# Moving layer 2's modulation rows to other stages, the rotary multiplies to VectorE, and one weight split ahead of the block sums, in a two-layer backbone step

## The chip, the cores and the metric

The kernel runs on one core of a Trainium2 chip. Its engines work side by side, each through its own queue in order: TensorE (PE in the profile; PEld is its weight load), VectorE (DVE), ScalarE (ACT), GpSimd (POOL), and SyncE (SP), which here only issues transfers. The metric is the time of one execution on the device, in microseconds (us); lower is better. All data are float32.

## What is computed

One inference step of a backbone with two layers, width 1024, for 512 latent ("sample") and 128 context ("prompt") tokens. Layer 1 of the text (index 0) mixes with a gated DeltaNet and a long convolution, layer 2 (index 1) with two kinds of attention, one over all keys (mixer C, with normed q and k) and one over a window of 128 (mixer D). Each layer ends in a gated feed-forward net (ConvFFN) with 2816 inner channels. Every sub-layer takes a shift, a scale and a gate, the layer's six *modulations*, from the conditioning vector:

```python
def modulation(cvec, w_mod, b_mod):
    m = jax.nn.silu(cvec) @ w_mod + b_mod
    return jnp.split(m[:, None, :], 6, axis=-1)

def apply_rope_2d(x, cos, sin):
    ...
    out = jnp.stack([x1 * c - x2 * s, x2 * c + x1 * s], axis=-2).reshape(B, L, H, HD)

# each layer: x += gate * mixer(rmsnorm(x) * (1 + scale) + shift) @ w_out
#             x += gate * (silu(dwconv(h @ w_up_a)) * (h @ w_up_b)) @ w_dn
```

(The two comment lines sum up the trunk.) The six modulations of a layer are 6 x 1024 numbers for each of two conditioning vectors.

## The kernel before

The residual stream lies transposed in four tiles `x`, channels on partitions, 642 columns (both groups of tokens and two spare columns). Each float32 operand of a large product is split into a rounded high part and a rest (`split_w`: a copy on ScalarE gives `wwh`, a subtraction on VectorE `wwl`), and `mm3` (lines 307 to 311) sends three matmuls for every product: high by high (L309), high by rest (L310) and rest by high (L311). TensorE is thereby the engine with most work, and VectorE makes the rests it needs.

The stages come in this order: modulations of layer 1 and its mixers (to about 640 us of the span), layer 1's output projection, layer 1's feed-forward net in three groups (`FGROUPS`: 8, 7 and 7 tiles of inner channels), q/k/v projections of layer 2 by `od_unit`, attention, layer 2's output projection, layer 2's feed-forward net. A projection back to the residual is `project_out`: eight output tiles `d`, each in two column halves `out(d, w, hf)`, and behind each half `residual` (L445) on VectorE adds gate times result into `x`. Where a norm follows (`then`), the last four tiles' weights are split first and run half by half, with `sq` (ScalarE) and `acc` (L439, VectorE) adding up squares and `nr` (L394, GpSimd) taking the root.

**Modulation rows.** Layer 1's modulations are computed on TensorE at the start. Those of layer 2 are computed on VectorE by `mod_rows`, as multiply-and-accumulate instructions over 128x512 pieces (L256, `mjunk`) of the transposed weight (`mraw`, from `w_modT`), with the conditioning rows (`crow`) spread over partitions. Chunk `ch` of six is one of the modulations; a chunk is 32 such instructions. `mod_rows` is a generator: each `next` issues one piece of the load and its 4 (pieces of 1024) or 2 (pieces of 512) instructions. `LANES` says which chunks are made beside which stage. The pieces beside a `project_out` are drawn by its argument `between`, those beside the projections of layer 2 by the loop over `units(range(4))` (one piece in every third step), and those beside attention by `merge`, which interleaves generators by their costs; the last number of each of its pairs is the total cost a generator is taken for.

```python
LANES = (((0,), (1,), (2,)), (3, 4), (5,))     # groups of layer 1's FFN; layer 2's projections and attention; its output projection
```

**Rotation.** `od_post` is queued for each 128-token tile of q, k or v: a copy out of PSUM to `oy`, for mixer C a norm (ScalarE squares L1703, VectorE L1704, GpSimd root, VectorE L1709), and for q and k of latent tokens the rotary position: two multiplies of 128x128 elements into `ot` on GpSimd (L1718), one of 128x256 on VectorE (L1721), and the sum on VectorE (L1725). Then TensorE transposes the tile (L1734) and ScalarE copies it out. Each `yield` lets the steps of other tiles go first.

**Feed-forward start.** The net's input product is a block scheme on 2x2 blocks (seven products instead of eight) for all tiles but the first two, which run as `plain_unit`. Its operands are block sums made by `combine`; weights of a block tile are made by `block_weights` (loads, sums, and splits `cwh` on ScalarE, `cwl` on VectorE, L579/L580), one split for each `next`. The products of a block tile are named `bx`, `by`, `bv` after the PSUM bank they add into, those of a plain tile `pu`.

The program is written as one sequence; a scheduler then orders each engine's queue by readiness and priority, so what is written in another place may come out in another order on an engine. SP issues its loads strictly in its queue's order: a load whose buffer is still in use holds up the ones behind it.

## Time and profile before

| | us |
|---|---|
| median of three executions | 1896.49 |
| lowest, highest | 1892.93, 4376.39 |
| the profiled execution | 1896.52 |
| its span, first to last instruction | 1894.7 |

The span is what the profile shows; 1.8 us of that execution lie around it. The stages, by the times at which their lines run (us from the span's start):

| stage | from, to |
|---|---|
| layer 1's output projection | 640, 690 |
| layer 1's FFN: norm, two plain tiles, block tiles and three groups | 690, 1150 |
| layer 2's q/k/v projections of mixer C, with the norm and the rotation | 1150, 1222 |
| attention, with the projections of mixer D | 1222, 1380 |
| layer 2's output projection | 1380, 1424 |
| layer 2's FFN and final norm | 1424, 1895 |

In the profile a line such as "L1721 DVE ... x12 | 5.1, 425 | 8.7 <-POOL ot" is a group: 12 instructions of source line 1721 on VectorE, 5.1 us busy, 425 ns each on average, and 8.7 us in which the engine sat idle just before them, waiting for GpSimd's `ot`. Rows of waits say which instruction of which engine was waited for, the total, the number of times and the longest. Rows of the timeline give start, duration, engine, line, and in brackets the idle time before and who ended it. PEclk is the clock that TensorE was granted, as a share of full speed. Buffer numbers are left out of names.

### The profile page before, as it was taken

The numbers are of one execution on the slowest core, as the hardware profiler recorded it, in microseconds if no ns is written. First come the engines' busy times: TensorE is split into PE (matmuls) and PEld (weight loads), VectorE is DVE, ScalarE is ACT, GpSimd is POOL, SyncE is SP. The second block draws the span as 40 slices with busy tenths as digits, with TensorE's granted clock in tenths as the row PEclk, the third lists the DMA queues.
The fourth block names the chain that finished last, engine by engine and source line by source line (L and its number), as shares of the span: only waits on it lengthen the run. The fifth ranks groups of instructions, "written<-read, shape, count | busy, mean of one in ns | idle before, by whom it ended". The sixth has DMA issues, their size and how long they took to land. (4 is left out here: it accounts for less than half of the span.)

```text
span 1894.7 us, 31530 instructions
## 1 busy us (share of the span) xinstructions
PE 1790.8 (95%) x12052; PEld 1666.0 (88%) x12052; DVE 1366.1 (72%) x2848; ACT 846.6 (45%) x1676; POOL 338.5 (18%) x397
## 2 busy tenths in 40 slices
PE   5899999999889999999999998899999999999998
PEld 1578899998667899999989998877899999999997
DVE  4755666667887759777777888796777873774774
ACT  3555443433232346624624635444536651552653
POOL 2313432324554100000000004310001000000001
PEclk9899999999989999999999999999999999999999
DMA  8322112224544613564564554431242461552631
GB/s 283 124 98 91 34 58 73 66 69 140 173 167 148 200 51 81 156 191 123 143 190 130 161 174 154 145 116 35 96 167 73 129 156 57 142 144 76 158 93 56
DMA packets 86929, 233.15 MB, mean 123 GB/s; under 512 B 9176, under 2 KB 20824, under 8 KB 86650
## 3 DMA queue, kind: packets, MB, share of 16 engines
q1 hardware_dynamic: 66976, 191.40, 30.8%
q0 software_dynamic: 5760, 20.97, 6.7%
q10 hardware_dynamic: 14042, 18.76, 2.8%
q8 instruction: 95, 1.56, 0.3%
q14 instruction: 56, 0.46, 0.1%
HBM read 214.56 MB, written 16.54 MB: 122 GB/s over the span
## 5 line engine op out<-in xcount | busy, mean ns | idle before, releaser
L579 ACT CAST cwh<-wr 128x512 fp32r<-128x512 f32 x200 | 119.6, 620 | 152.4 <-PE bx L310 43.6
L303 ACT CAST wwh<-wr 128x1024 fp32r<-128x1024 f32 (+1 forms) x100 | 101.3, 1013 | 182.7 <-PE mm L310 116.0
L580 DVE TENSOR_TENSOR cwl<-wr,cwh 128x512 fp32r<-128x512 f32 x200 | 133.4, 686 | 39.1 <-ACT cwh L579 38.8
L445 DVE SCALAR_TENSOR_TENSOR x<-mm,mod,x 128x128 f32<-128x128 f32 (+3 forms) x192 | 77.4, 435 | 107.8 <-PE mm L311 107.7
L304 DVE TENSOR_TENSOR wwl<-wr,wwh 128x1024 fp32r<-128x1024 f32 (+1 forms) x100 | 122.1, 1223 | 44.1 <-ACT wwh L303 43.4
L309 PE MATMUL mm<-h0h,wwh 128*128 128x384 f32 (+2 forms) x448 | 148.8, 332 | 0.5 <-DVE d L845 0.2
L591 POOL DMA_DIRECT2D t<-in_w_up x40 | 35.0, 874 | 604.9 <-DMA t<-in_w_up 248.5
L310 PE MATMUL mm<-h0l,wwh 128*128 128x384 f32 (+2 forms) x448 | 140.3, 313 | 0.0
L311 PE MATMUL mm<-h0h,wwl 128*128 128x384 f32 (+2 forms) x448 | 139.4, 311 | 0.0
L256 DVE SCALAR_TENSOR_TENSOR mjunk<-mraw,crow 128x512 f32<-128x512 f32 x192 | 126.7, 691 | 6.0 <-DMA mraw<-in_w_modT 5.7
L309 PE MATMUL od<-owh,h2h 128*128 128x256 f32 x320 | 97.3, 307 | 0.6 <-ACT h2h L428 0.6
L679 DVE SCALAR_TENSOR_TENSOR cv<-ab,par,cv 128x641 f32<-128x641 f32 x88 | 77.7, 883 | 26.3 <-ACT cv L677 25.5
L311 PE MATMUL od<-owh,h2l 128*128 128x256 f32 x320 | 91.3, 289 | 2.2 <-DVE h2l L429 1.3
L310 PE MATMUL od<-owl,h2h 128*128 128x256 f32 x320 | 91.8, 288 | 0.4 <-DVE owl L1613 0.4
L1134 POOL TENSOR_TENSOR am<-a,msk 128x512 fp32r<-128x512 f32 x60 | 72.8, 1221 | 92.4 <-PE Q L1163 81.2
L309 PEld LDWEIGHTS mm<-h0h,wwh 128*128 128x128 f32 x448 | 85.4, 191 | 3.1 <-issue 1.8
L310 PEld LDWEIGHTS mm<-h0l,wwh 128*128 128x128 f32 x448 | 84.9, 190 | 0.6 <-issue 0.2
L311 PEld LDWEIGHTS mm<-h0h,wwl 128*128 128x128 f32 x448 | 84.6, 189 | 0.1
L721 DVE SCALAR_TENSOR_TENSOR cv<-mm,par,cv 128x382 f32<-128x382 f32 (+2 forms) x96 | 52.1, 544 | 32.8 <-ACT cv L715 32.0
L436 ACT ACTIVATE sq<-x 128x320 f32<-128x320 f32 (+4 forms) x63 | 31.5, 501 | 83.8 <-DVE x L445 75.8
L579 ACT CAST cwh<-t 128x512 fp32r<-128x512 f32 x80 | 48.1, 623 | 41.7 <-PE bx L310 17.4
L310 PEld LDWEIGHTS od<-owl,h2h 128*128 128x128 f32 x320 | 61.4, 192 | 4.3 <-issue 3.6
(556 smaller groups left out, 6184.1 us busy)
## 6 DMA issues: line engine op xcount, KB each, us to landing
wr<-in_w_mod SPq DMA_DIRECT2D x48, 512.0 KB, 4.6
wr<-in_w_up SPq DMA_DIRECT2D x48, 512.0 KB, 4.1
t<-in_w_up SPq DMA_DIRECT2D x80, 256.0 KB, 3.2
t<-in_w_up POOLq DMA_DIRECT2D x40, 512.0 KB, 6.4
mraw<-in_w_modT SPq DMA_DIRECT2D x32, 512.0 KB, 5.1
wr<-in_w_in SPq DMA_DIRECT2D x28, 512.0 KB, 3.3
wr<-in_w_dn SPq DMA_DIRECT2D x32, 448.0 KB, 3.4
wr<-in_w_up SPq DMA_DIRECT2D x40, 256.0 KB, 3.5
```

Of the source, the lines that this page charges most:

```text
L256: nc.vector.scalar_tensor_tensor(out=junk, in0=w[:, c : c + 512], scalar=1.0, in1=rows[m][:, c0 + c : c0 + c + 512], op0=ALU.mult, op1=ALU ...
L303: nc.scalar.copy(hi[:, :K], src)
L304: nc.vector.tensor_tensor(out=lo[:, :K], in0=src, in1=hi[:, :K].bitcast(F32), op=ALU.subtract)
L309: nc.tensor.matmul(ps, l[0](k), r[0](k), start=start, stop=False, skip_group_check=more)
L310: nc.tensor.matmul(ps, l[0](k), r[1](k), start=False, stop=False, skip_group_check=more)
L311: nc.tensor.matmul(ps, l[1](k), r[0](k), start=False, stop=stop, skip_group_check=more)
L445: nc.vector.scalar_tensor_tensor(out=xt[:, a:b], in0=ps[:, a - c0 : b - c0], scalar=mcol(layer, ch, d, m), in1=xt[:, a:b], op0=ALU.mult, o ...
L579: nc.scalar.copy(hi, src)
L580: nc.vector.tensor_tensor(out=lo, in0=src, in1=hi.bitcast(F32), op=ALU.subtract)
L679: nc.vector.scalar_tensor_tensor(out=t[:, c0:c1], in0=ar[:, c0 + s_ : c1 + s_], scalar=w[i], in1=t[:, c0:c1], op0=ALU.mult, op1=ALU.add)
L721: nc.vector.scalar_tensor_tensor(out=t[:, c0:c1], in0=p[:, c0 + s_ - a : c1 + s_ - a], scalar=w[i], in1=t[:, c0:c1], op0=ALU.mult, op1=ALU ...
L1134: eng.tensor_tensor(out=v(out), in0=v(a32), in1=msk[:, lv, :, None, :].broadcast_to([P, 2, 2, P]), op=ALU.mult)
```

## The change

Five edits that the diff shows, of which the first two decide where a row of modulations is made:

- `LANES` becomes one list for all stages. Layer 1's output projection, which had no such work, makes chunk 0; the three groups of layer 1's FFN make chunks 1, 2 and 3; attention makes chunk 4 only; layer 2's output projection makes chunk 5, as before. The loop that drew pieces during `units(range(4))` is gone.
- `project_out` draws a piece after a tile's two halves and no longer ahead of its weights (where there is no norm behind, it drew two pieces ahead of each of the first two tiles); in the last four tiles it draws one after the first half's product.
- The two rotary multiplies run on VectorE; `oy` has six buffers, `ot` one.
- Every tile waits one step more ahead of its transposes (only q of mixer C did).
- In the feed-forward start, the third tile's `block_weights` and its first two splits stand between the two `combine` calls' parts, and that tile's `up_unit` is called inside the branch.

```diff
@@ -1,5 +1,6 @@
 import math
 from contextlib import ExitStack
+from itertools import chain
 
 import numpy as np
 
@@ -61,7 +62,7 @@
 RATE = 1.0
 
 
-LANES = (((0,), (1,), (2,)), (3, 4), (5,))
+LANES = ((0,), ((1,), (2,), (3,)), (4,), (5,))
 
 
 PCOL = {}
@@ -476,18 +477,17 @@
 
         first = KD - 4 if then else KD
         for d in range(first):
-            for _ in range(2 if d < 2 and not then else 1):
-                next(between, None)
             w = ws[d] if d < len(ws) else split_w(load_raw(wsrc(d), K), K)
             for hf in range(2):
                 out(d, w, hf)
+            next(between, None)
 
         ws = [split_w(load_raw(wsrc(d), K), K) for d in range(first, KD)]
         for hf in range(2):
             for d, w in zip(range(first, KD), ws):
+                q = out(d, w, hf)
                 if hf == 0:
                     next(between, None)
-                q = out(d, w, hf)
                 if hf == 1 and d == first:
                     norm_stats(acc, rb, 0, cut=cut)
                 if hf == 1 and d == first + soon:
@@ -622,7 +622,7 @@
                 yield
         give(f, ar, br, 1.0)
 
-    def up_unit(layer, f, B, pool, outs, give):
+    def up_unit(layer, f, B, pool, outs, give, ws=None):
 
 
         def product(ps, n, st):
@@ -635,7 +635,7 @@
             nc.scalar.copy(q, ps[:, :ST])
             return q
 
-        ws = block_weights(layer, f, pool)
+        ws = ws or block_weights(layer, f, pool)
         ar, br = (outs[f % 2][:, i, :] for i in range(2))
         X, Y = bank("d", "bx"), bank("mm", "by")
         product(X, "a11", True)
@@ -693,10 +693,15 @@
                 us = [plain_unit(*pre[2 * f : 2 * f + 2], f, B, outs, give) for f in range(2)]
                 for u in us:
                     next(u)
-                for k, u in zip((0, 2), us):
-                    combine(B, k)
-                    next(u, None)
-                f1 = 2
+                combine(B, 0)
+                next(us[0], None)
+
+                ws = block_weights(layer, 2, pool)
+                early = [next(ws) for _ in range(2)]
+                combine(B, 2)
+                next(us[1], None)
+                up_unit(layer, 2, B, pool, outs, give, chain(early, ws))
+                f1 = 3
             for f in range(f1, f0 + n):
                 up_unit(layer, f, B, pool, outs, give)
             project_out(
@@ -1597,7 +1602,7 @@
         B = Blocks(gstack.enter_context(tc.tile_pool(name=f"g{layer}", bufs=8)))
         pool = gstack.enter_context(tc.tile_pool(name=f"b{layer}", bufs=2))
         take, pre = to_blocks(x, layer, B)
-        between = rows_beside(LANES[2], pool) if layer else iter(())
+        between = rows_beside(LANES[3 * layer], pool)
         project_out(x, mix, layer, 2, wout(layer), KD, take, between=between, ws=ws, cut=SCUT, soon=3)
         return B, pool, gstack, pre
 
@@ -1632,7 +1637,7 @@
             for i in range(4):
                 nc.scalar.dma_start(xs[:, 2 * i : 2 * i + 2, :], x[i])
 
-    ffn_blocks(x, B, bpool, 0, to_attention, None, gstack, pre, LANES[0])
+    ffn_blocks(x, B, bpool, 0, to_attention, None, gstack, pre, LANES[1])
     h = h2
 
 
@@ -1694,7 +1699,7 @@
             if t == 4:
                 nc.sync.dma_start(O["new_v"][mixer], dst)
             return
-        y = od.tile([P, 256], F32, tag="oy", name=nm("oy"), bufs=5)
+        y = od.tile([P, 256], F32, tag="oy", name=nm("oy"), bufs=6)
         nc.scalar.copy(y, ps)
         if mixer == 0:
             sq = tmp.tile([P, NT], F32, tag="fs", name=nm("osq"))
@@ -1711,11 +1716,11 @@
                     in1=gains[:, 0 if part < 2 else 1, :], op0=ALU.mult, op1=ALU.mult,
                 )
         if t < 4:
-            t2 = od.tile([P, 256], F32, tag="ot2", name=nm("ot2"))
+            t2 = od.tile([P, 256], F32, tag="ot2", name=nm("ot2"), bufs=1)
             q4 = lambda ap: ap.rearrange("p (h g x c) -> p h g x c", h=2, g=2, x=2)
             r4 = lambda ap: ap.rearrange("p (g x c) -> p g x c", g=2, x=2)[:, None].broadcast_to([P, 2, 2, 2, 32])
             for i in range(2):
-                nc.gpsimd.tensor_tensor(
+                nc.vector.tensor_tensor(
                     out=q4(t2)[:, :, :, i, :], in0=q4(y)[:, :, :, 1 - i, :], in1=r4(rope[:, 1, t, :])[:, :, :, i, :], op=ALU.mult
                 )
             nc.vector.tensor_tensor(
@@ -1727,8 +1732,7 @@
             nc.sync.dma_start(O["new_k"][mixer], y)
         yield
         yield
-        if u < 2:
-            yield
+        yield
         pt = s_ps("ot")
         for i in range(2):
             nc.tensor.transpose(pt[:, BLK[i]], y[:, BLK[i]], ident)
@@ -1970,12 +1974,10 @@
                     yield c
 
     lanes = mod_rows(
-        LANES[1], lambda: od.tile([P, 1024], F32, tag="crow", name=nm("crow")),
+        LANES[2], lambda: od.tile([P, 1024], F32, tag="crow", name=nm("crow")),
         lambda: od.tile([P, 512], F32, tag="mraw", name=nm("mraw"), bufs=3), 512,
     )
-    for n, _ in enumerate(units(range(4))):
-        if n % 3 == 2:
-            next(lanes)
+    run(units(range(4)))
     lend["by"] = None
     att["pool"] = odv.enter_context(tc.tile_pool(name="att", bufs=2))
     identb = att["pool"].tile([P, P], BF16, tag="identb", name="identb", bufs=1)
@@ -1989,7 +1991,7 @@
             pattern=[[s_, P]], channel_multiplier=-s_,
         )
     att_all = all_heads()
-    merge((units((4, 6, 7, 5)), 54.0), (until_none(att_all), AW), (lanes, 29.5))
+    merge((units((4, 6, 7, 5)), 54.0), (until_none(att_all), AW), (lanes, 24.8))
     lend["by"] = "attention"
     for _ in att_all:
         step()

```

What the scheduler makes of it is seen in each engine's order. On SP, in the second group of layer 1's FFN: `mraw` are the modulation pieces, `wr<-in_w_dn` the output projection's weights. Before:

```order
L298 DMA wr_9863<-in_w_dn 128x896
L298 DMA wr_9926<-in_w_dn 128x896
L251 DMA mraw_9603<-in_w_modT 128x1024
L251 DMA mraw_9664<-in_w_modT 128x1024
L251 DMA mraw_9672<-in_w_modT 128x1024
L251 DMA mraw_9733<-in_w_modT 128x1024
L251 DMA mraw_9794<-in_w_modT 128x1024
L251 DMA mraw_9855<-in_w_modT 128x1024
L251 DMA mraw_9916<-in_w_modT 128x1024
L298 DMA wr_9979<-in_w_dn 128x896
L298 DMA wr_10032<-in_w_dn 128x896
```

and now (line numbers are one higher):

```order
L299 DMA wr_9911<-in_w_dn 128x896
L299 DMA wr_9972<-in_w_dn 128x896
L252 DMA mraw_9781<-in_w_modT 128x1024
L252 DMA mraw_9842<-in_w_modT 128x1024
L252 DMA mraw_9903<-in_w_modT 128x1024
L299 DMA wr_10033<-in_w_dn 128x896
L252 DMA mraw_9964<-in_w_modT 128x1024
L252 DMA mraw_10025<-in_w_modT 128x1024
L299 DMA wr_10094<-in_w_dn 128x896
L252 DMA mraw_10086<-in_w_modT 128x1024
```

Before, seven modulation loads in a row stood ahead of the last two weight loads; now no more than three stand ahead of the next weight.

On VectorE, in layer 1's output projection, around the weight of its fourth tile: `x<-mm` is the residual (`mm_6288` and `mm_6315` are the halves of the first tile before), `acc` the sum of squares, `wwl` the rest of a weight (`wwl_6470` is the fourth tile's before). Before:

```order
L304 TENSOR_TENSOR wwl_6405<-wr_6402,wwh_6404 128x1024
L445 SCALAR_TENSOR_TENSOR x_6272<-mm_6288,mod,x_6272 128x320
L445 SCALAR_TENSOR_TENSOR x_6272<-mm_6315,mod,x_6272 128x192
L445 SCALAR_TENSOR_TENSOR x_6272<-mm_6315,mod,x_6272 128x128
L304 TENSOR_TENSOR wwl_6470<-wr_6467,wwh_6469 128x1024
L304 TENSOR_TENSOR wwl_6535<-wr_6532,wwh_6534 128x1024
L445 SCALAR_TENSOR_TENSOR x_6272<-mm_6343,mod,x_6272 128x320
L439 TENSOR_TENSOR acc_6286<-acc_6286,sq_6369 128x320
L445 SCALAR_TENSOR_TENSOR x_6272<-mm_6372,mod,x_6272 128x192
L445 SCALAR_TENSOR_TENSOR x_6272<-mm_6372,mod,x_6272 128x128
L304 TENSOR_TENSOR wwl_6541<-wr_6538,wwh_6540 128x1024
```

and now, where `mm_6430` and `mm_6459` are the halves of the third tile and `wwl_6500` is the fourth tile's rest:

```order
L446 SCALAR_TENSOR_TENSOR x_6273<-mm_6430,mod,x_6273 128x320
L257 SCALAR_TENSOR_TENSOR mjunk_6421,mpart<-mraw_6416,crow_6344 128x512
L440 TENSOR_TENSOR acc_6286<-acc_6286,sq_6456 128x320
L257 SCALAR_TENSOR_TENSOR mjunk_6491,mpart<-mraw_6489,crow_6343 128x512
L257 SCALAR_TENSOR_TENSOR mjunk_6494,mpart<-mraw_6489,crow_6343 128x512
L257 SCALAR_TENSOR_TENSOR mjunk_6491,mpart<-mraw_6489,crow_6344 128x512
L446 SCALAR_TENSOR_TENSOR x_6273<-mm_6459,mod,x_6273 128x192
L446 SCALAR_TENSOR_TENSOR x_6273<-mm_6459,mod,x_6273 128x128
L257 SCALAR_TENSOR_TENSOR mjunk_6494,mpart<-mraw_6489,crow_6344 128x512
L440 TENSOR_TENSOR acc_6286<-acc_6286,sq_6486 128x322
L305 TENSOR_TENSOR wwl_6500<-wr_6497,wwh_6499 128x1024
```

The fourth tile's rest stood behind the first tile's residuals; now it stands behind the third tile's second residual, a modulation instruction and a sum, that is, behind work that the third tile's last matmuls set free.

On VectorE, in layer 2's projections, one tile's norm and rotation. Before:

```order
L256 SCALAR_TENSOR_TENSOR mjunk_12052,mpart<-mraw_12050,crow_11827 128x512
L1721 TENSOR_TENSOR oy_11990<-oy_11990,rope 128x256
L256 SCALAR_TENSOR_TENSOR mjunk_12052,mpart<-mraw_12050,crow_11828 128x512
L1725 TENSOR_TENSOR oy_11990<-oy_11990,ot_2086_12037 128x256
L1709 SCALAR_TENSOR_TENSOR oy_12041<-oy_12041,ors_12048,gains 128x128 x2
L1704 TENSOR_SCALAR oss_12094<-oss_12094 128x2
L256 SCALAR_TENSOR_TENSOR mjunk_12115,mpart<-mraw_12113,crow_11827 128x512
L1721 TENSOR_TENSOR oy_12041<-oy_12041,rope 128x256
L256 SCALAR_TENSOR_TENSOR mjunk_12115,mpart<-mraw_12113,crow_11828 128x512
L1725 TENSOR_TENSOR oy_12041<-oy_12041,ot_2095_12087 128x256
```

and now:

```order
L1723 TENSOR_TENSOR ot_2094_12037<-oy_12000,rope 128x4x32 x2
L1714 SCALAR_TENSOR_TENSOR oy_12041<-oy_12041,ors_12048,gains 128x128
L1726 TENSOR_TENSOR oy_12000<-oy_12000,rope 128x256
L1709 TENSOR_SCALAR oss_12095<-oss_12095 128x2
L1709 TENSOR_SCALAR oss_12140<-oss_12140 128x2
L1730 TENSOR_TENSOR oy_12000<-oy_12000,ot_2094_12037 128x256
L1714 SCALAR_TENSOR_TENSOR oy_12092<-oy_12092,ors_12099,gains 128x128
L1723 TENSOR_TENSOR ot_2104_12088<-oy_12041,rope 128x4x32 x2
L1714 SCALAR_TENSOR_TENSOR oy_12092<-oy_12092,ors_12099,gains 128x128
L1726 TENSOR_TENSOR oy_12041<-oy_12041,rope 128x256
```

The modulation pieces between the steps are gone, and the pair of multiplies that GpSimd made stands on VectorE (L1723). Chunk 4's 32 instructions stand further on: one ahead of the first tile and three among the rotated tiles, then 18 almost without a break in the rows where unit 3 runs (the v tiles, which have neither norm nor rotation), with the splits of unit 4's weights (`owl`) at the end of that stretch, and 10 among the attention's.

## The prediction

> **What bounds the kernel now.** I read the page first (busy times), then the windows by stage, then the waits of TensorE in each window, and the timelines around the longest of them.
>
> ```profile
> PE 1790.8 (95%) x12052; PEld 1666.0 (88%) x12052; DVE 1366.1 (72%) x2848; ACT 846.6 (45%) x1676; POOL 338.5 (18%) x397
> ```
> TensorE is busy 95% of the span, and the change takes no matmul away. It can only move the remaining 5%, some 104 us, together with matmuls that run at a lower clock. So I look where the edits touch, for TensorE's waits and its granted clock.
>
> ```profile
> core 0: us, PE busy (x) PEld busy (x) DVE busy (x) ACT busy (x) POOL busy (x), PEclk, DMA share, GB/s
> 640.00:705.00 65.00, 62.37 (x408) 60.88 (x408) 36.93 (x72) 25.02 (x44) 3.36 (x7) 0.97 0.35 119
> 973.00:979.00 6.00, 2.58 (x8) 2.58 (x9) 6.00 (x18) 0.00 (x0) 0.00 (x0) 0.76 0.61 206
> 1170.00:1222.00 52.00, 42.33 (x320) 39.34 (x321) 41.77 (x126) 23.94 (x87) 28.11 (x44) 0.97 0.33 107
> 1222.00:1340.00 118.00, 113.02 (x729) 90.73 (x728) 90.29 (x278) 53.39 (x145) 12.13 (x22) 0.99 0.27 86
> 1472.00:1482.00 10.00, 6.63 (x29) 6.37 (x28) 9.24 (x17) 4.37 (x8) 0.00 (x0) 0.66 0.06 23
> ```
> Four places leave TensorE idle: one stall in the feed-forward net's second group (973), layer 2's projections (9.67 us idle of 52), attention (4.98 of 118) and one stall at layer 2's feed-forward start (1472). Layer 1's output projection has VectorE at 37 of 65 us: there is the room that the change fills.
>
> **The second group's stall (973).**
>
> ```profile
> 971.46 0.28 PE L310 MATMUL mm<-g01l,wwh 128*128 128x258 f32 x1
> 976.42 0.69 PE L311 MATMUL mm<-g01h,wwl 128*128 128x384 f32 x1 [4.67 <-DVE wwl L304]
> ...
> 979.46 0.37 PE L311 MATMUL mm<-g01h,wwl 128*128 128x384 f32 x1
> 979.67 0.34 PE L309 MATMUL mm<-g01h,wwh 128*128 128x384 f32 x1
> 979.85 0.34 PE L310 MATMUL mm<-g01l,wwh 128*128 128x384 f32 x1
> ```
> ```profile
> 956.33 19.39 SPq L251 DMA_DIRECT2D mraw<-in_w_modT  x7
> 976.39 3.78 SPq L298 DMA_DIRECT2D wr<-in_w_dn  x2
> ```
> TensorE waits for a weight's rest, which stands on VectorE behind modulation instructions; seven modulation loads hold SP from 956 to 976 with two weight loads behind them. From start to start the gap is 976.42 - 971.46 = 4.96, where 0.12 is usual: 4.8 lost. After it ten matmuls start in 979.67 - 976.42 = 3.25 us, where ten steps of 0.18 (979.67 to 979.85) make 1.8: 1.45 more at the lower clock. In the new order no weight stands behind more than three modulation loads, and each weight's split stands on VectorE at least one tile ahead of its use. The cover is that one tile of matmuls; without it the next weight would stall likewise. I take -6.0 of the 6.25 (bounds: 0, if another weight is late instead, and -6.25).
>
> At this place the Trainium skill (TensorE: Matmul & The Clock Gate, "HAM oscillation") says that an idle gap of more than about 3.4 us halves TensorE's clock, for about 3.4 us of work. This agrees with the rows here on when it happens, a wait of 2.47 us without and of 3.37 and 4.67 us with slow matmuls behind it (rows below and above). It would price each at 1.7 us, an estimate from that page, where the rows give 1.45 here and 2.4 below; by the page the sum would come out 0.45 us higher.
>
> **Layer 2's projections (1170 to 1222).**
>
> ```profile
> PE ot L1734 <- DVE oy L1725: 5.0, 6, 1.4
> PE ot L1734 <- ACT osq L1703: 2.0, 2, 1.1
> L256 DVE SCALAR_TENSOR_TENSOR mjunk<-mraw,crow 128x512 f32<-128x512 f32 x25 | 17.2, 694 | 0.0
> L1709 DVE SCALAR_TENSOR_TENSOR oy<-oy,ors,gains 128x128 f32<-128x128 f32 x30 | 9.6, 346 | 1.5 <-POOL ors L193 1.5
> L1721 DVE TENSOR_TENSOR oy<-oy,rope 128x256 f32<-128x256 f32 x12 | 5.1, 425 | 8.7 <-POOL ot L1718 8.7
> L1704 DVE TENSOR_SCALAR oss<-oss 128x2 f32<-128x2 f32 x14 | 2.5, 191 | 0.0
> L1718 POOL TENSOR_TENSOR ot<-oy,rope 128x128 f32<-128x128 f32 x24 | 16.5, 709 | 14.9 <-DVE oss L1704 14.5 <-DVE oy L1709 0.4
> 1198.03 0.28 PE L309 MATMUL od<-owh,h2h 128*128 128x256 f32 x1
> 1198.14 0.28 PE L310 MATMUL od<-owl,h2h 128*128 128x256 f32 x1
> ```
> Transposes wait for a chain: VectorE's norm, GpSimd's pair of multiplies (2 x 0.71 us), VectorE again, with modulation instructions between. VectorE itself idles 8.7 us for GpSimd. Undisturbed, a matmul starts about every 0.118 us, so the window's 320 need 37.8 us and 14.2 of its 52 are lost. Other waits of that list, for splits and copies out, make 3.0 and stay; 11.2 hang on the chain.
>
> Of the edits, the loop's removal takes up to 25 modulation instructions off (17.2 us of VectorE); the pair costs VectorE 24 multiplies of 128x128, which the trace does not show on it. The nearest row is L1709 of that size, 0.346 with a scalar operand: 0.35 each, 8.4 us (bounds: 0.2, the L1704 row of two columns, and 0.43, L1721 of twice the size). A rotated tile then costs VectorE 0.19 + 2 x 0.35 + 2 x 0.35 + 0.43 + 0.43 (L1725, as L1721) = 2.45 us against 24 x 0.118 = 2.83 us of matmuls: VectorE keeps up. One step more before the transposes costs TensorE nothing, since matmuls of the next tile stand there; it needs the sixth `oy`. The wait for GpSimd's root stays. I take -11 (bounds: 0, if the modulation burst behind the rotated tiles makes up new waits, to -14.2).
>
> **Attention (1222 to 1340).**
>
> ```profile
> PE tr L1004 <- ACT oy L1698: 2.4, 1, 2.4
> L256 DVE SCALAR_TENSOR_TENSOR mjunk<-mraw,crow 128x512 f32<-128x512 f32 x40 | 27.8, 708 | 4.0 <-DMA mraw<-in_w_modT 3.8
> L1721 DVE TENSOR_TENSOR oy<-oy,rope 128x256 f32<-128x256 f32 x11 | 4.6, 418 | 6.1 <-POOL ot L1718 4.5 <-ACT mxh L1763 1.6
> 1252.66 0.62 DVE mjunk L256 x2
> 1253.30 3.08 DMA mraw<-in_w_modT
> ```
> The last two rows are of the chain that ended last, which at this place runs through modulation instructions on VectorE and the load of one. Of 40, ten remain: 30 x 0.71 = 21 us less; 22 multiplies of 0.35 = 7.7 us more; the waits for GpSimd (4.5) go. But most of this is beside other work: TensorE idles 4.98 us, and 1% of clock is 1.2. I take -4 of these 6.2 (bounds -6.2 and +3: the ten instructions and eleven pairs stand ahead of softmax steps on VectorE that TensorE's transposes wait for, 10 x 0.71 + 7.7 = 15 us, of which a fifth may show).
>
> **The feed-forward starts.**
>
> ```profile
> 734.54 0.41 PE L311 MATMUL by<-a12h,cwl 128*128 128x320 f32 x1 [2.47 <-DVE cwl L580]
> 714.00:741.00 27.00, 24.53 (x168) 24.24 (x167) 26.77 (x43) 18.63 (x34) 0.00 (x0) 1.00 0.04 13
> 1475.73 0.63 PE L311 MATMUL bx<-a11h,cwl 128*128 128x320 f32 x1 [3.37 <-DVE cwl L580]
> ...
> 1481.23 0.33 PE L309 MATMUL bx<-s2h,cwh 128*128 128x320 f32 x1
> 1481.84 0.31 PE L310 MATMUL bx<-s2l,cwh 128*128 128x320 f32 x1
> 1481.99 0.31 PE L311 MATMUL bx<-s2h,cwl 128*128 128x320 f32 x1
> ```
> In layer 1 VectorE is busy 26.77 of the 27 us: it does combinations and splits without a pause. Taking two splits forward moves the combinations back by as much, so the 2.47 wait stands at another product of the same tile: 0 (bounds -2.5, +1). In layer 2 the wait is the tile's very first split: 3.37, after which 21 matmuls take 1481.23 - 1475.73 = 5.5 us, where 21 x 0.147 = 3.1. The first two splits now lie ahead; the later wait should be that of layer 1, 2.5, short of what brought the low clock: -(3.4 - 2.5) - 2.4 = -3.3 (bounds 0 and -5.8).
>
> **Layer 1's output projection: what is added.**
>
> ```profile
> L304 DVE TENSOR_TENSOR wwl<-wr,wwh 128x1024 fp32r<-128x1024 f32 x9 | 11.0, 1220 | 5.7 <-ACT wwh L303 5.6
> L445 DVE SCALAR_TENSOR_TENSOR x<-mm,mod,x 128x320 f32<-128x320 f32 (+2 forms) x20 | 8.4, 447 | 12.1 <-PE mm L311 12.0
> L439 DVE TENSOR_TENSOR acc<-acc,sq 128x320 f32<-128x320 f32 (+1 forms) x11 | 5.4, 491 | 4.4 <-ACT sq L436 4.4
> L256 DVE SCALAR_TENSOR_TENSOR mjunk<-mraw,crow 128x512 f32<-128x512 f32 x32 | 20.7, 686 | 1.9 <-DMA mraw<-in_w_modT 1.9
> PE rb L402 <- POOL nr L394: 0.3, 1, 0.3
> PE rb L402 <- POOL nr L394: 0.9, 1, 0.9
> ```
> (The first three rows are of 640 to 690, the fourth of layer 2's output projection, where the same 32 instructions already run without holding TensorE; the last two are the norm behind each projection, layer 1's first.) VectorE has 65 - 37 = 28 us for 20.7. But the fourth tile's rest now stands behind the third tile's second residual: two pieces of residual (0.9), one modulation instruction (0.7), a sum (0.5) and the rest itself (1.2) pass after that tile's last matmul, 3.3 us, while eight matmuls that need only high parts go ahead (1.2): +2.1. The transfers `t` of the block tiles move behind the modulations on SP and POOL, as in layer 2 already; there the root `nr` on GpSimd stands behind an accumulating transfer, and its wait is 0.9 instead of 0.3: +0.6. Eight modulation loads and two of `crow` go past four `x` and four weight loads on SP; they are hidden, since the fourth weight is needed six half tiles (6 x 24 x 0.147 = 21 us) after the first. Together +2.7 (bounds 0 and +9: if a modulation load lands late on VectorE's queue, each weight behind it waits as at 973, 6.25). Groups one and three and layer 2's output projection, with as much work as before in nearly the same order: 0.
>
> **Sum.** -6.0 - 11 - 4 - 3.3 + 0 + 2.7 = -21.6; against the profiled execution's 1896.5 that is 1874.9. Its span is 1894.7 with 1.8 around it, and it lies within 0.1 of the median of 1896.49, so I take the sum for the median too. About 2% (38 us) is what a measurement of this kernel can tell from no change; the forecast lies inside.
>
> **Rivals.**
> - *Waits only move.* The 18 modulation instructions in a row (14 us with their reads) run as fast as their loads land through three buffers; a load of this kind cost VectorE 3.08 in one place. Behind them stand the splits of the next unit's weights, so TensorE waits there, and the projections gain 3, attention 0: -6 - 3 - 3.3 + 2.7 = -9.6, 1886.9. For it: VectorE's queue is in order; against it: v tiles leave VectorE nothing else to do.
> - *All goes.* Projections -14.2, attention -6.2, both starts -2.5 and -5.8, the added work hidden: -6.25 - 14.2 - 6.2 - 8.3 = -35, 1861.5. Against it: VectorE's own instructions in the third window (41.8 - 17.2 + 8.4 = 33 of 52 us) must then hide wholly. The Trainium skill (SBUF — State Buffer, "Who interferes with whom") has GpSimd and VectorE lock each other out at a shared port, so that VectorE would get time back for each multiply taken off GpSimd. The rows agree little: `mjunk` takes 694 ns beside the multiplies and 686 in layer 2's output projection without them.
> - *Layer 1's output projection becomes the stall.* Its weights come through the same SP queue as eight new loads. If the five weights four to eight each wait as the one at 973 (6.25), that is +31 in place of +2.7, and the whole is +7: 1903.5. It decides from four late weights on (25 against the 24.3 gained). Against it: the new order lets no more than four modulation loads stand ahead of a weight.
> - *Rotation makes VectorE the bound* (0.43 for each multiply and 25 modulation instructions still in that window): the window stays at 52 us, attention +3, total -6 + 3 - 3.3 + 2.7 = -3.6, 1892.9.
>
> **Chances.** Forecast 0.52 (its own range 1867 to 1883), waits only move 0.20, all goes 0.12, rotation the bound 0.06, output projection the stall 0.10. The range 1860 to 1893 holds all but the last and tails, 8 in 10 and a little more. Faster by over 2% (below 1858.6) needs more than all the bounds: 0.04. Slower by over 2% (above 1934.4) needs more than five such weights: 0.02. Within 2%: 0.94.
>
> **What would show it.** No `wwl` wait near the second group's fifth tile, and PEclk 1.00 there; no `ot` waits for `oy` in the projections and no GpSimd rows of the rotation; TensorE's wait at layer 2's feed-forward start below 3 us at full clock, and layer 1's still near 2.5; a new wait of about 2 us for `wwl` in layer 1's output projection. I am wrong if VectorE's 18 instructions in a row are followed by a wait of TensorE for `owl`, if a multiply on VectorE takes over 0.45 us, or if layer 1's output projection shows several waits for weights.

## The result, and the profile after

| | before | with the change |
|---|---|---|
| median, us | 1896.08 (4 executions) | 1879.21 (4, from 1878.37 to 1880.43) |
| span of the profiled execution, us | 1894.7 | 1878.7 |

The ratio is 0.9908, 95% interval 0.9889 to 0.9926: about 17 us (14 to 21) less, inside the 2%, with an interval that is clear of no change. Of the four executions before, one took 4376.39 us, and the ratio is taken without it. The forecast was 1874.9, in a range of 1860 to 1893. A second measurement of the same kernel gave 0.9922 (0.9898 to 0.9946).

The same views as before, of the changed kernel: the page's busy times, windows at the places that correspond, and TensorE's waits there. Line numbers are one to five higher.

```profile
PE 1788.3 (95%) x12052; PEld 1665.0 (89%) x12052; DVE 1374.1 (73%) x2896; ACT 848.1 (45%) x1678; POOL 311.4 (17%) x349
```
```profile
core 0: us, PE busy (x) PEld busy (x) DVE busy (x) ACT busy (x) POOL busy (x), PEclk, DMA share, GB/s
967.00:973.00 6.00, 6.00 (x43) 6.00 (x42) 5.86 (x17) 0.87 (x1) 0.00 (x0) 1.00 0.57 183
1165.60:1209.00 43.40, 40.29 (x325) 38.33 (x324) 37.55 (x124) 23.15 (x89) 16.00 (x21) 1.00 0.31 100
1209.00:1327.00 118.00, 113.99 (x731) 91.72 (x730) 83.21 (x262) 53.67 (x147) 0.40 (x1) 0.97 0.19 61
1459.00:1467.00 8.00, 5.93 (x29) 5.40 (x28) 8.00 (x15) 3.68 (x7) 0.00 (x0) 0.79 0.04 13
```
```profile
PE tr L1009 <- ACT oy L1703: 3.7, 1, 3.7
...
PE bv L312 <- DVE cwl L580: 3.6, 2, 1.8
...
PE mm L312 <- DVE wwl L305: 2.0, 1, 2.0
...
PE ot L1738 <- DVE oy L1730: 1.5, 3, 0.6
...
PE ot L1738 <- ACT osq L1708: 0.6, 1, 0.6
```
The reader is to see three things. The second group's stall is gone: TensorE is busy 6.00 of 6.00 us at full clock. Layer 2's projections take 43.4 us for what took 52, with 2.1 us of waits for `oy` and `osq` in place of 7.0. And at attention's start the wait for `oy`, 2.4 us before, is now 3.7, at a granted clock of 0.97 (0.99 before), although VectorE has 7 us less to do there than before (83.21 against 90.29).

To see where the time went I use that TensorE runs the same 12,052 matmuls in every trace. A stage is the time from the start of one numbered matmul to that of another, read from TensorE's timeline, so that a stage can be compared wherever it lies in the span. Some matmuls stand in another order after an edit, so a stage's bounds can lie a few matmuls off.

| stage, by its time in the span before | before | change | change, second profile |
|---|---|---|---|
| start, 4 to 133 | 129.4 | 125.2 | 129.9 |
| layer 1's mixers, 133 to 531 | 397.7 | 397.6 | 397.8 |
| their last part, 531 to 600 | 68.6 | 70.3 | 65.1 |
| up to layer 1's output projection and through it, 600 to 681 | 81.6 | 84.5 | 82.2 |
| norm and plain tiles, 681 to 722 | 40.8 | 40.4 | 40.8 |
| layer 1's feed-forward start, 722 to 762 | 40.0 | 42.3 | 41.2 |
| groups one and two, 762 to 955 | 193.5 | 193.7 | 192.3 |
| second group's output, 955 to 988 | 32.8 | 26.4 | 26.4 |
| third group, norm, 988 to 1161 | 173.1 | 173.2 | 174.0 |
| layer 2's projections, 1161 to 1229 | 67.9 | 58.5 | 58.5 |
| attention, 1229 to 1380 | 150.8 | 150.2 | 148.9 |
| layer 2's output projection and norm, 1380 to 1450 | 70.6 | 69.8 | 70.6 |
| layer 2's feed-forward start, 1450 to 1496 | 45.7 | 43.9 | 42.4 |
| the rest, 1496 to 1884 | 387.3 | 386.8 | 387.7 |

Two profiles of one program differ by 4.7 us at the start and by 5.2 us in the last mixer part, which the edits do not touch; what the table shows there is no effect of the change. The rest is: 6.3 less at the second group, 9.4 less in the projections, 2 to 3 less at layer 2's feed-forward start, 1 to 2 more at layer 1's, 1 to 3 more around layer 1's output projection, and 1 to 2 less at attention.

### The profile page after: what moved, and what is told of

Read it like the earlier page. It is cut to its first block, busy times and chain, and to the rows that moved or that the text cites. A ratio compares the mean times of both kernels' runs of the same rounds, so it can differ in the third digit from the quotient of the medians.

```text
span 1878.7 us, 31471 instructions
## 1 busy us (share of the span) xinstructions
PE 1788.3 (95%) x12052; PEld 1665.0 (89%) x12052; DVE 1374.1 (73%) x2896; ACT 848.1 (45%) x1678; POOL 311.4 (17%) x349
## 4 chain that ended last, share of the span: by engine, by line
PE 72%; DVE 13%; ACT 3%; POOL 3%; issue 2%; DMA 2%; POOLq 0%; DVEq 0%; ACTq 0%
PE mm L310 10%; PE mm L312 10%; PE mm L311 10%; PE bx L310 4%; PE bx L311 4%; PE bx L312 4%; PE bv L312 2%; PE bv L310 2%; PE bv L311 2%; PE tr L1009 2%; PE fx L1395 1%; PE YT L1176 1%; PE Y L1174 1%; PE Q L1168 1%; PE o L1872 1%
## 5 line engine op out<-in xcount | busy, mean ns | idle before, releaser
L305 DVE TENSOR_TENSOR wwl<-wr,wwh 128x1024 fp32r<-128x1024 f32 (+1 forms) x100 | 122.2, 1223 | 39.4 <-ACT wwh L304 38.6
L1139 POOL TENSOR_TENSOR am<-a,msk 128x512 fp32r<-128x512 f32 x60 | 73.0, 1225 | 92.4 <-PE Q L1168 81.2
L312 PEld LDWEIGHTS mm<-h0h,wwl 128*128 128x128 f32 x448 | 84.5, 189 | 0.1
L310 PEld LDWEIGHTS od<-owh,h2h 128*128 128x128 f32 x320 | 60.4, 189 | 4.5 <-issue 4.2
```

Source lines behind the costliest of these rows:

```text
L305: nc.vector.tensor_tensor(out=lo[:, :K], in0=src, in1=hi[:, :K].bitcast(F32), op=ALU.subtract)
L310: nc.tensor.matmul(ps, l[0](k), r[0](k), start=start, stop=False, skip_group_check=more)
L312: nc.tensor.matmul(ps, l[1](k), r[0](k), start=False, stop=stop, skip_group_check=more)
L1139: eng.tensor_tensor(out=v(out), in0=v(a32), in1=msk[:, lv, :, None, :].broadcast_to([P, 2, 2, P]), op=ALU.mult)
```

## The experiments

Stage lengths in us, as in the table above; each run is one profile. "Draw order" is `project_out`'s edit, "placement" the edits of `LANES` and of the draws beside the projections and attention. The experiments come from three chips, on which the kernel before took 1892.35, 1896.67 and 1898.33 us, so total times are compared as ratios to it, and a difference between stages counts for little where two profiles of the change differ by as much (2.3 us at the output projection, 1.5 at layer 2's start, 1.3 at attention).

| run | output projection (600 to 681) | layer 1's start | second group | projections | attention | layer 2's start |
|---|---|---|---|---|---|---|
| before | 81.6 | 40.0 | 32.8 | 67.9 | 150.8 | 45.7 |
| the change | 84.5 | 42.3 | 26.4 | 58.5 | 150.2 | 43.9 |
| rotation back on GpSimd | 84.4 | 41.1 | 26.4 | 60.9 | 158.1 | 43.9 |
| third tile undone | 82.1 | 43.0 | 26.4 | 58.5 | 150.1 | 44.9 |
| draw order alone | 81.6 | 40.2 | 26.4 | 66.4 | 152.7 | 44.9 |
| rotation and third tile alone | 82.3 | 40.6 | 32.9 | 60.1 | 147.0 | 43.9 |
| draw order and rotation | 81.8 | 39.4 | 26.4 | 60.1 | 145.1 | 45.8 |
| draw order, rotation, third tile | 81.1 | 41.0 | 26.4 | 60.1 | 145.6 | 43.8 |
| the change, chunk 4 spread | 82.1 | 41.0 | 26.4 | 60.2 | 145.3 | 43.9 |
| the change, weights ahead | 79.8 | 41.0 | 26.4 | 58.5 | 150.3 | 42.4 |
| the last three, three splits early | 81.1 | 37.4 | 26.4 | 60.1 | 146.7 | 40.4 |

**Rotation back on GpSimd.**

```diff
-                nc.vector.tensor_tensor(
+                nc.gpsimd.tensor_tensor(
                     out=q4(t2)[:, :, :, i, :], ...
```


> The changed kernel with the two rotary multiplies back on GpSimd (and the two tiles' buffers as before); the placement of the modulations, the extra step and the third tile stay changed. Theory: the transposes' waits of before came from two things in one chain, the hop to GpSimd and the modulation instructions between its steps, about half each. Of the 9.4 us that layer 2's projections gained (from 1161 to 1229 us of the span before), 3 to 5 come back, as TensorE's waits for oy and VectorE's idle time for ot. Rival A: the modulation instructions alone did it; then the stage stays within 1 us of the changed kernel's, although VectorE idles for GpSimd again. Rival B: the hop alone did it; then 8 us or more come back.

Of the projections' 9.4 us, 2.4 came back, a little less than the theory's 3 to 5: with the modulation instructions gone, the hop to GpSimd alone costs little. This run keeps the extra step ahead of the transposes; whether the hop would cost little without it was not tried. Attention, of which nothing was expected, became 7.9 us longer, nearly all of it by one wait, for `pl`, the exponentials of the softmax. From the waits and from VectorE's timeline of this run (start, duration, engine, line, in brackets the idle time before):

```profile
PE tr L1009 <- ACT pl L1848: 11.0, 1, 11.0
```
```profile
1214.50 0.69 DVE L257 SCALAR_TENSOR_TENSOR mjunk<-mraw,crow 128x512 f32<-128x512 f32 x1 [1.19 <-DMA mraw<-in_w_modT]
...
1219.74 0.69 DVE L257 SCALAR_TENSOR_TENSOR mjunk<-mraw,crow 128x512 f32<-128x512 f32 x1 [1.35 <-DMA mraw<-in_w_modT]
...
1223.05 1.22 DVE L1618 TENSOR_TENSOR owl<-wr,owh 128x1024 fp32r<-128x1024 f32 x1
1224.19 0.68 DVE L257 SCALAR_TENSOR_TENSOR mjunk<-mraw,crow 128x512 f32<-128x512 f32 x1
1224.80 1.22 DVE L1618 TENSOR_TENSOR owl<-wr,owh 128x1024 fp32r<-128x1024 f32 x1
1225.93 0.68 DVE L1835 TENSOR_REDUCE mx<-sc 128x4 f32<-128x512 f32 x1
```
Modulation instructions in a row, held twice by their loads, stand ahead of unit 4's weight splits and of the first softmax step (`mx`). TensorE, out of other work, waits 11 us. The change has the same row of instructions, held by a load for 0.94 us, with a wait of 3.7; the first and the last of it, in its timeline:

```profile
1204.58 0.69 DVE L257 SCALAR_TENSOR_TENSOR mjunk<-mraw,crow 128x512 f32<-128x512 f32 x1
...
1217.54 0.68 DVE L257 SCALAR_TENSOR_TENSOR mjunk<-mraw,crow 128x512 f32<-128x512 f32 x1
1218.15 1.22 DVE L1618 TENSOR_TENSOR owl<-wr,owh 128x1024 fp32r<-128x1024 f32 x1
1219.28 0.68 DVE L1835 TENSOR_REDUCE mx<-sc 128x4 f32<-128x512 f32 x1
```
From 1204.6 to 1219.3 VectorE makes nothing that attention's first step can use.

**Third tile undone.**

```diff
-                combine(B, 0)
-                next(us[0], None)
-                ws = block_weights(layer, 2, pool)
-                early = [next(ws) for _ in range(2)]
-                combine(B, 2)
...
+                for k, u in zip((0, 2), us):
+                    combine(B, k)
+                    next(u, None)
```


> The changed kernel with the third tile's weights made after the combinations again, as before. Theory: in layer 1's feed-forward start the edit lost about 2.3 us (two waits and slow matmuls behind them in place of one wait of 2.5 at full clock) and in layer 2's it won about 1.8 us; undone, the first start is 2.3 us shorter with one wait of 2.5 for by at full clock, the second 1.8 us longer with a first wait of 3.4 and slow matmuls; 0.5 us less in all. Rival: whether slow matmuls follow a wait of 2 to 3.4 us is chance from run to run; then the waits come out as said, but the slow matmuls may stand at other places or not at all.

Layer 2's start behaved nearly as said: 1.0 us longer instead of 1.8, with one wait of 3.4. Layer 1's start did not: 0.7 us longer, not 2.3 shorter. Its waits, without the third tile's edit and (below) with it:

```profile
732.57 0.63 PE L312 MATMUL bx<-a11h,cwl 128*128 128x320 f32 x1 [3.38 <-DVE cwl L580]
```
```profile
733.96 0.42 PE L310 MATMUL by<-a12h,cwh 128*128 128x320 f32 x1 [0.27 <-ACT cwh L579]
...
736.33 0.54 PE L312 MATMUL bv<-s1h,cwl 128*128 128x320 f32 x1 [1.81 <-DVE cwl L580]
736.67 0.47 PE L310 MATMUL bv<-s1h,cwh 128*128 128x320 f32 x1
736.93 0.47 PE L310 MATMUL bx<-s2h,cwh 128*128 128x320 f32 x1
```
In this run, with the placement changed, layer 1's start waits for the first split, as layer 2's did before; without the placement (draw order alone, draw order and rotation) it is the 2.5 us wait of before. VectorE's queue shows why: in this run the first two rests (`cwl`) stand behind both combinations and most of the plain tiles' steps, while in "draw order and rotation", which differs by the placement alone, the first one stands among them. From the two timelines, this run first:
```profile
731.83 1.29 DVE L580 TENSOR_TENSOR cwl<-wr,cwh 128x512 fp32r<-128x512 f32 x2
```
```profile
725.85 0.69 DVE L579 TENSOR_TENSOR cwl<-wr,cwh 128x512 fp32r<-128x512 f32 x1
```
So the placement alone makes layer 1's start 43.0 instead of 39.4 us, and the third tile's edit then takes 0.7 to 2.0 us of it back. Without the placement the same edit costs about 1 us (40.6 to 41.0 with it, 39.4 to 40.2 without it): with the edit the start takes 40.6 to 42.3 us, with or without the placement.

**Draw order alone**, on the kernel before.

```diff
         for d in range(first):
-            for _ in range(2 if d < 2 and not then else 1):
-                next(between, None)
...
             for hf in range(2):
                 out(d, w, hf)
+            next(between, None)
```


> The kernel before with one edit: project_out draws a modulation piece after a tile's halves instead of ahead of its weights; all chunks stay where they were. Theory: this alone takes the 4.7 us wait for the weight's rest in the second feed-forward group away, since no more than three modulation loads then stand ahead of a weight on SP; 6.2 us less there, and everything else within 1 us of before. Rival: the wait depended on which groups held which chunks (how far VectorE was behind); then a wait of 3 us or more for wwl is still there.

6.3 us less at the second group, no wait: the theory holds. The edit moves the weights on SP and on VectorE together; which of the two queues held them was not separated. Elsewhere single stages moved by up to 2 us, where 1 was expected. One of these is attention, 1.9 us longer, and its wait at the start is longer than that of the change:
```profile
PE tr L1003 <- ACT oy L1697: 4.3, 1, 4.3
```
Here no row of 18 stands on VectorE: ahead of the first softmax step there are 11 modulation instructions with weight splits between them, as in the kernel before, whose wait is 2.4. So such a row is not the only thing that makes this wait.

**Rotation and third tile alone**: `LANES`, the draws and `project_out` as before.

```diff
-LANES = ((0,), ((1,), (2,), (3,)), (4,), (5,))
+LANES = ((), ((0,), (1,), (2,)), (3, 4), (5,))
...
-    run(units(range(4)))
+    for n, _ in enumerate(units(range(4))):
+        if n % 3 == 2:
+            next(lanes)
```


> The changed kernel with the modulations where they were before, drawn as before; the rotation on VectorE, the extra step and the third tile stay changed. Theory: the projections' gain needs VectorE's room; with 25 modulation instructions still there a rotated tile costs VectorE about 4 us against 2.83 us of matmuls, so the stage is no faster than before, within 2 us, and TensorE's waits for oy stay near 5 us or grow. Rival: the hop to GpSimd was the limit; then the stage gains 5 us or more although the modulations are still there. Layer 1's output projection has no wait for wwl (2.0 us less than the changed kernel) and the second group's wait of about 4.7 us is back.

The theory fell. With all the modulation instructions still there the projections gained 7.8 us, and attention 3.8. VectorE kept up. The rest came as said: the second group's wait is back, and layer 1's output projection has none for `wwl`.

**The change again**, as a yardstick.


> The changed kernel itself once more, as a measure of what differs between two profiles of one program. Theory: the parts at the changed places repeat within 0.5 us (layer 1's output projection with one 2.0 us wait for wwl, the second group without a wait, layer 2's projections at 58.5 us, attention at 150.2), while the start (up to 133 us), the last mixer stage (531 to 600) and the length of the slow matmuls behind the third tile's waits differ by 1 to 4 us. Rival: the last mixer stage is again 1.7 us longer than before, so that it belongs to the change.

The waits repeat (2.0 for `wwl`, 3.5 at attention). The last mixer part was 5.2 us shorter this time, so it is chance. Layer 1's output projection and layer 2's start were 2.3 and 1.5 us shorter with the same waits: after them no matmuls ran at the lower clock, which explains the 1.5 and about 1.5 of the 2.3. Attention, 1.3 us shorter, repeated less closely than expected.

**Draw order and rotation**, and **the same with the third tile**: the kernel before with these edits alone, chunks where they were. Beside the draw order's diff above, the first has

```diff
-                nc.gpsimd.tensor_tensor(
+                nc.vector.tensor_tensor(
                     out=q4(t2)[:, :, :, i, :], ...
...
-        if u < 2:
-            yield
+        yield
```


> The kernel before with two of the edits: the new draw order in project_out, and the rotation on VectorE with its buffers and the extra step. All chunks stay where they were, the third tile too. Theory: placing the chunks elsewhere is no gain in itself: second group -6.3, projections -7.8, attention -3.8 as with rotation and third tile alone, layer 1's output projection and feed-forward start as before; about -18 against before, some 4 us faster than the whole change. Rival: the moved chunks matter beside attention; then it is no faster than the whole change (-14).

> The kernel before with the draw order, the rotation and the third tile's edit: the whole change without the placement of the chunks. Theory: like draw order and rotation alone, and with the third tile's edit layer 2's feed-forward start 1 us shorter (two waits of 0.4 and 2.0 in place of one of 3.5), the stretch ahead of layer 1's output projection 0.8 us longer and layer 1's start within 1 us: about -18 against before. Rival: the third tile's edit gains in both layers' starts (2 us or more against the run without it).

They measured 1876.25 us, ratio 0.9890 (0.9867 to 0.9914), and 1874.63, 0.9881 (0.9858 to 0.9903). Both ratios lie below that of the whole change, 0.9908 (0.9889 to 0.9926), but the intervals overlap, so that they are faster is not shown by the times. By the stages the placement gives nothing: it gains 1.6 us in the projections and loses 3 to 5 in attention. Between 1225 and 1340 us of the first of these runs the full load of modulations stands on VectorE,

```profile
L256 DVE SCALAR_TENSOR_TENSOR mjunk<-mraw,crow 128x512 f32<-128x512 f32 x32 | 21.3, 683 | 0.2
```
and attention still takes 145.1 us. Between these two profiles, the third tile gained 2.0 in layer 2's start and lost 1.6 in layer 1's.

**Chunk 4 spread**, on the whole change.

```diff
-    run(units(range(4)))
+    for n, _ in enumerate(units(range(4))):
+        if n % 3 == 2:
+            next(lanes, None)
...
-    merge(..., (lanes, 24.8))
+    merge(..., (lanes, 4.65))
```


> The whole change, with chunk 4 drawn during the projections in every third step, as chunks 3 and 4 were before, and only its last three pieces beside attention. Theory: the 3.7 us wait at attention's start comes from the 18 modulation instructions in a row ahead of the first softmax steps on VectorE; spread over the rotated tiles they leave it free: attention 145 to 147 us in place of 150.2, projections 1 to 2 us longer (about 60), the sum 2 to 4 us shorter. Rival: the wait at attention's start is set by something else (the norm of unit 4's tiles on ScalarE, which the wait names); then attention stays at 150 and the projections lose 1.5.

As the theory said: attention 145.3, projections 60.2, together 3.2 less than with the change (1.9 less than its second profile). The one execution took 1878.47 us, which does not tell it from the change; the gain is seen in the stages alone. The wait at attention's start is 1.6 instead of 3.7, and the granted clock behind it stays at 1.00, where in the change it is 0.85 in the 12 us around the wait:

```profile
PE tr L1009 <- ACT pl L1848: 1.6, 1, 1.6
```

**Weights ahead**, on the whole change, in `project_out`:

```diff
             for hf in range(2):
                 out(d, w, hf)
+            if d + 1 == len(ws) < first:
+                ws = [*ws, split_w(load_raw(wsrc(d + 1), K), K)]
             next(between, None)
```


> The whole change, with layer 1's output projection splitting the weight of its third and fourth tile ahead of the modulation piece drawn in front of them. Theory: the 2.0 us wait for wwl there is the fourth tile's rest standing behind the third tile's residual on VectorE; with the rest ahead of it the wait is gone and the stage is 2.3 us shorter (3 to 3.5 if slow matmuls had followed the wait), all else as in the change. Rival: the weight's load or its ScalarE copy is late too, behind the modulation loads on SP; then a wait for wwl or wwh of 1 us or more stays.

The wait for `wwl` is gone and the stage 2.4 us shorter than the change's second profile. But the norm and plain tiles behind it took 43.1 us instead of 40.8, against the expectation that all else would stay: TensorE's wait for `nr` rose from 0.3 to 1.3,

```profile
PE rb L403 <- POOL nr L395: 1.3, 1, 1.3
```
and 13 matmuls at the lower clock followed. Most of what the edit saved was lost there. Why `nr` came later was not tried.

**Three splits early**, on draw order, rotation and third tile:

```diff
-                early = [next(ws) for _ in range(2)]
+                early = [next(ws) for _ in range(3)]
```


> Draw order, rotation and third tile as in the run of these three, with three of the third tile's splits ahead of the second combination instead of two. Theory: the two waits at both feed-forward starts (0.4 and 2.0 us lost) are for the third split, which stood behind the second combination and the second plain tile's gate on VectorE; made early, 1 to 1.5 us less in each layer's start, and no slow matmuls behind: 2 to 4 us less than the run with two. Rival: VectorE is busy without a pause there, so the wait only moves on to the block sums or the fourth split, within 0.5 us of the run with two.

1871.0 us, ratio 0.9852 (0.9833 to 0.9872), the lowest ratio of all, and its interval lies wholly below that of the whole change (it overlaps that of the run with two splits). Layer 1's start is 3.6 us shorter than in the run with two and layer 2's 3.4, more than the 2 to 4 us in all that were expected: in each, the two waits became one of 0.4, and no matmul ran at the lower clock.

```profile
PE bv L312 <- DVE cwl L580: 0.4, 1, 0.4
```

**Without the extra step**, on draw order, rotation and third tile:

```diff
         yield
         yield
-        yield
+        if u < 2:
+            yield
```


> Draw order, rotation and third tile, without the extra step ahead of the transposes (only q of mixer C has it, as before). Theory: with the rotation on VectorE a tile's chain is short enough, and the step matters only for k of mixer C and the tiles of mixer D: projections and attention together within 1 us of the run with it (60.1 and 145.6 us). Rival: without it TensorE's transposes wait for oy again, 2 us or more in the two stages.

60.9 and 145.3 us against 60.1 and 145.6: the step is worth nothing that these profiles can show.

## Why the prediction was right, step by step

- **Second group: right.** Forecast -6.0, measured -6.3 in every run with the draw order, and by that edit alone.
- **Projections: size nearly right (-11 against -9.4), reason half right.** I took the chain and the modulation instructions for one cause of which both halves were needed, so that the size came out near is in part luck. With the rotation on VectorE and the modulations still in, it is -7.8 already (-7.0 without the extra step); with the modulations out and the rotation on GpSimd it is -7.0, but that run has the extra step and the new draw order too (the latter alone gives -1.5), so the modulations' own share is not shown. What is missing to -11 is the 2.1 us of waits for `oy` and `osq` that stayed. The multiply was priced at 0.35 us by its nearest row; it takes 0.28:

```profile
L1723 DVE TENSOR_TENSOR ot<-oy,rope 128x128 f32<-128x128 f32 x24 | 5.8, 284 | 0.0
```
  The rival "rotation makes VectorE the bound" asked for 0.43 us a multiply and 25 modulation instructions still there; "rotation and third tile alone" has the second without the first, and the stage became faster. The prediction's remark that `mjunk` hardly suffers beside GpSimd's multiplies rests on a mean of mostly undisturbed ones: in the trace of before, the 19 that ran beside a multiply took 746 ns on average and those beside no work of GpSimd 685, while the multiplies took from 448 to 1384 ns.
- **Attention: wrong by 2 to 3.5 us.** The failing step is "I take -4 of these 6.2", which rested on 30 modulation instructions fewer. Their number there does not matter (145.1 us with the full load). What gained was the rotation (-3.8 to -5.7); what gave most of it back was the row of 18 instructions ahead of attention, since the same kernel with them spread takes 145.3. This is the mechanism of "waits only move", which I had given 0.20 and a narrower victim: the weights' splits alone, where the first softmax step behind them is late too. The wait of 4.3 in "draw order alone", without that row, stays unexplained.
- **Feed-forward starts: layer 2's wait right, the clock and layer 1 wrong.** In layer 2 the wait did fall, from 3.4 to 0.3 and 1.8 at later products (2.5 was forecast). "Short of what brought the low clock" failed: behind the 1.8 us wait matmuls ran at the lower clock in the first profile (-1.8 in all) and not in the second (-3.3, as forecast). They did so in six of the eight profiles with these two splits early, so the hit in the second is luck. In layer 1 I forecast 0 and got +1.2 to +2.3. The failing step is that the wait of 2.5 "stands at another product of the same tile": it became two, of 0.3 and 1.8, with slow matmuls behind them in seven of eight profiles, and this costs about 1 us even without the placement. I had also kept the wait of 2.5 as given, but the new placement makes it 3.4 where the third tile's edit is missing.
- **Layer 1's output projection: right.** The forecast wait for the fourth tile's rest was 2.1 us; it is 2.0, and vanishes when the rest stands earlier. The wait for `nr` (+0.6) did not rise in the change; it rose by 1.0 where the stall ahead of it was removed. Net, +2.7 was forecast and +2.9 and +0.6 came; about 1.5 of the 2.9 are slow matmuls, which were not forecast. The 0.6, with a wait of 2.0, means that something ahead of it became some 1.5 us shorter. Three short waits among the projection's first products (`wwh`, `mixh` and `mixl`, 0.2 to 0.3 us each, around 640 us) stand in every run without the placement and in none with it. How the placement removes them was not tried.
- **Sum.** The profile of the change gave -16.0, of which -4.2 at the start and +1.7 in the last mixer part are chance; the second profile gave -21.2 by span. The medians' -17 stands between. The terms mis-sized are attention (2 to 3.5 us too much), the projections (1.6 too much) and layer 1's start (1 to 2 too little): all three forecast too much gain, and the sum missed the measured median by 4 us on that side.

## What to carry to other kernels

Work put beside an engine that has time left still stands somewhere in that engine's queue: a row of filler instructions directly ahead of the first step of the next stage cost 4 to 5 us there, while the same instructions spread out cost 1.6 in the stage before. When a stage shows a wait made of two things, do each edit alone before keeping both: here two edits (draw order, rotation) carried the gain and moving the chunks gave nothing. And a stall that is moved a little earlier is a gain only when its successor is gone too: two splits early moved the wait, three left 0.4 us of it.

## What the hardware showed that was not expected

How long TensorE stops does not alone decide whether it runs slower afterwards. At the two feed-forward starts, the output projection and the norm behind it, the same stops occur in many of these profiles. Measured from start to start, with a slow step 0.27 us instead of 0.15 between matmuls of 320 columns:

| stop before | profiles' places | followed by a row of 11 or more slow steps |
|---|---|---|
| one of 1.4 to 2.0 us (`tr`, ahead of the output projection) | 13 | 0 |
| one of 1.6 us (`nr`, weights ahead) | 1 | 1 |
| one of 2.35 us (`wwl`) | 5 | 2 |
| one of 2.8 us | 3 | 0 |
| 0.58 and then 2.1 us | 16 | 13 |
| one of 3.7 us | 5 | 5 |

So stops well under 3.4 us are followed by the lower clock, for 11 to 13 steps in a row (2.9 to 3.6 us, with 1.5 to 1.7 us lost), against 12 to 22 after the long stop (1.5 to 2.8 us lost), and the same program had it at one place in one profile and not in the next. The Trainium skill (TensorE: Matmul & The Clock Gate, "HAM oscillation") puts the limit at about 3.4 us; the runs here decide, and show it after a stop of 1.6 us already, in one place, and in 13 of 16 after 2.1 us when a shorter stop came just before. The page also says (Part 1) that the window in which activity is judged runs freely, which would fit the chance from profile to profile; no run here shows the window itself.
